# Operands laid out by the host: a two-layer streaming encoder whose cached keys, first input and some weights arrive feature-major, and whose other weights arrive in contiguous blocks

## The chip, the cores and the metric

The kernel runs on one core of a Trainium2 chip. The metric is the device time of one execution in microseconds, the median of the runs shown. All arithmetic is in 32 bits; matrix products are made from split operands (below).

## The reference, cut to what matters

Two token streams pass through the same two layers: a prompt of 512 frames, and a sample of 8 running streams with 16 new frames each, which also attends to 1024 cached positions.

```
D_MODEL = 1024; SEQ = 512; DEPTH = 2; DEC_BATCH = 8; DEC_SEQ = 16; PAST_LEN = 1024
G_A = 4; H_B = 4; NOPE_DIM = 128; ROPE_DIM = 64; Q_LORA = 384; KV_LORA = 256; H_C = 4; D_C = 64

def trunk_layer(x, q_pos, past, ...):
    p = x @ w_in
    a_u, a_v, b_cq, b_ckv, b_kr, c_q, c_k, c_v = jnp.split(p, in_split_points(), axis=-1)
    u = jax.nn.gelu(a_u); v = layer_norm(jax.nn.gelu(a_v))
    y_a = spatial_gate(u, v, w_s, b_s)                     # w_s: 4 x 128 x 128, masked by chunk
    q = jnp.einsum('bsc,chd->bshd', rms_norm(b_cq, g_cq), w_uq)
    q_rope = rope(q[..., NOPE_DIM:], q_pos)
    q_lat = jnp.einsum('bshn,hcn->bshc', q[..., :NOPE_DIM], w_uk)
    ckv = rms_norm(b_ckv, g_ckv); krope = rope(b_kr, q_pos)
    # past: cached ckv (1024 x 256), krope (1024 x 64), stick-breaking k and v (1024 x 4 x 64)
    out_lat = softmax(q_lat . ckv_all + q_rope . kr_all) . ckv_all
    y_b = jnp.einsum('bshc,hcd->bshd', out_lat, w_uv)
    y_c = stick_breaking(c_q, k_all, v_all)
    y = concat(rms_norm(y_a), rms_norm(y_b), rms_norm(y_c))
    x = layer_norm(ALPHA * x + y @ w_out)
    h = jnp.square(jax.nn.relu(x @ w_up + b_up)) @ w_down + b_down
    return layer_norm(ALPHA * x + h), caches
```

The outputs are both streams after two layers and the new cache entries.

## The kernel before, in words

**Split products.** An operand is cut into a high half, rounded by a cast on ACT, and a low half, the rest, by a subtraction on DVE or POOL (`split`). A product is then three matmuls (`mm3`: high-high, high-low, low-high). For the sample's attention, the query's high and low halves are stacked as the 128 columns of the stationary operand, so two matmuls do (`block` in `sample_scores`), and `fold_to` adds the two halves of the result.

**Transposes.** TensorE contracts over partitions, so an operand must lie with its contracted feature along the partitions. What lies otherwise is turned by TensorE: a matmul with the identity writes the turned block to PSUM (`tr` for 32-bit data, `trr` for rounded data), and the split reads it from there. In the kernel before these are turned on chip: the input of each layer (`transpose_x`), the cached keys of both attentions (`cache_T`: two blocks of 128 keys by 256 features, four transposes, then a split from PSUM), the cached rotary keys (`kr_of` and `turned`: a split in SBUF with the low half made on POOL into `kds`, four transposes, one copy to `kr`), the spatial weights (`gm_weights`, four per call), and `w_uk` for the sample's queries (`s_prep`, eight per layer), besides attention weights and activations made on chip, which stay so.

**Two threads.** The prompt (P) runs `p_layer`: phase `in` (input projection), `mix` (gating, latents and the prompt's stick-breaking attention), `mla` (`lane_pmla`), `out` and `mlp` (`p_out_mlp`). The sample (S) runs `s_layer`: it waits for P's `mix`, then `s_prep`, latent attention (`lane_smla`), stick-breaking attention (`lane_ssb`), `out` and `mlp` (`s_out_mlp`). P's phase `in` of the second layer waits for S's end of the first layer, since it projects the sample's frames too. Both threads are generators; `weave` interleaves them in one program order. It keeps a credit in estimated TensorE time: S gets `RATE[phase of P]` (0.6 to 1.0 while both run) of what P gets, where both can go on. `Pace` estimates when each engine comes to an instruction; it knows ACT, DVE, POOL and TensorE costs, no DMA. Inside a thread, `lanes` interleaves generators in the same way. The order that comes out is each engine's order; nothing is reordered at run time, apart from what the scheduler of the framework does at build time.

**Sample attention.** `pipeline` runs `front` (scores) ahead of `back` (values) by two or three pairs of sequences. Per sequence and 512 keys, `front` loads keys in two half blocks of 256 KB (ring `rawK`, two buffers), turns and splits them to `cT`, and multiplies one half block behind; `back` loads values in two half blocks (ring `rawV`, two buffers), casts the high half on DVE and subtracts the low half on POOL (`cN`). Per layer that is 32 half blocks of keys and 32 of values in each of the two attentions.

**Queues.** Every DMA is issued by SP, in program order, so a transfer that waits for its buffer holds back those behind it. `load_w` (line 258) loads weights to the rings `rawP` (three buffers, four at the start) and `rawS`, `load_cache` (line 1082) the cached keys and values. In the profile almost all engine instructions carry line 109, that of the helper `Timed`, so groups are told apart by their tiles.

## Time and profile before

| | |
|---|---|
| median of 3 runs | 1838.31 us (1836.42 to 1840.13) |
| profiled execution, span from first to last instruction | 1839.0 us |
| profiled execution, mean granted TensorE clock | 0.983 |
| TensorE matmuls | 9756, busy 95% of the span |
| DVE, ACT, POOL busy | 69%, 51%, 20% |
| bytes by DMA | 300.54 MB, queue busy 52.5% of 16 engines' span |

The profiled execution's own time is its span. A busy time is the union of the instructions' own durations; TensorE matmuls overlap in its pipeline, so the mean duration of one is longer than the distance from start to start.

### The profile page before, as it was taken

Reading aid. Unit: us, or ns where it says so; the run is one execution under the profiler, and the core shown is the slowest. Engines: PE = TensorE matmul, PEld = TensorE weight load, DVE = VectorE, ACT = ScalarE, POOL = GpSimd, SP = SyncE. Lnnn points to the kernel's source line nnn. Section 1 sums busy time; section 2 is a strip of 40 time slices with the busy share of each in tenths; the row PEclk is TensorE's granted clock in tenths of the full one; section 3 lists DMA queues with packets and bytes.
Section 4 is the critical chain, followed back from the end, with each engine's and each line's share of the span. In section 5 each row is a group of like instructions: output and inputs, shape, how many; then the busy total and the mean of one; then the engine's idle time right before and its main releaser. Section 6 shows DMA issues by size and latency. Waiting matters only on the chain.

```text
span 1839.0 us, 26468 instructions
## 1 busy us (share of the span) xinstructions
PE 1753.1 (95%) x9756; PEld 1510.5 (82%) x9756; DVE 1277.6 (69%) x1845; ACT 938.2 (51%) x1652; POOL 363.0 (20%) x372
## 2 busy tenths in 40 slices
PE   8998998999999999999989989899899999999997
PEld 7887887888888778888778988888788888878886
DVE  3476777785676766767844767777766777677676
ACT  3474666343445434656525757663443463446561
POOL 0014123461012230000110231344402113110001
PEclk9998999999999999999999989999999999999999
DMA  6325556444355347768743245573444444677772
GB/s 209 119 73 155 154 176 172 139 135 142 112 153 167 92 131 230 254 213 269 229 141 113 77 143 171 162 221 101 152 155 138 138 150 130 198 220 244 229 229 102
DMA packets 240018, 300.54 MB, mean 163 GB/s; under 512 B 35088, under 2 KB 167312, under 8 KB 239888
## 3 DMA queue, kind: packets, MB, share of 16 engines
q1 hardware_dynamic: 239888, 298.85, 52.5%
q8 instruction: 77, 1.26, 0.3%
q14 instruction: 53, 0.43, 0.1%
HBM read 281.49 MB, written 17.30 MB: 162 GB/s over the span
## 4 chain that ended last, share of the span: by engine, by line
PE 68%; DVE 11%; DMA 8%; ACT 5%; issue 5%; POOL 2%; SPq 0%; DVEq 0%; POOLq 0%; ACTq 0%
PE acc L109 47%; PE sC L109 12%; PE x L109 8%; DMA rawV<-in_cache_mla_ckv_dram 3%; DMA rawP<-in_w_down_dram 2%; DVE w L109 2%; ACT w L109 2%; POOL cN L109 2%; DVE xy L109 2%; DVE a L109 1%; DVE wx L109 1%; DVE cN L109 1%; DVE m L109 1%; DMA rawK<-in_cache_mla_ckv_dram 1%; ACT a L109 1%
## 5 line engine op out<-in xcount | busy, mean ns | idle before, releaser
L109 PE MATMUL acc<-yT,wx 128*128 128x512 f32 (+1 forms) x1632 | 395.8, 386 | 0.4 <-DVE wx L109 0.2
L109 PE MATMUL acc<-w,hT 128*128 128x512 f32 x1536 | 391.3, 397 | 1.8 <-DVE xy L109 0.9
L109 PEld LDWEIGHTS acc<-yT,wx 128*128 128x128 f32 x1632 | 292.0, 191 | 59.0 <-DVE wx L109 1.5
L109 PEld LDWEIGHTS acc<-w,hT 128*128 128x128 f32 x1536 | 283.3, 188 | 66.0 <-DVE xy L109 2.3
L109 POOL TENSOR_TENSOR cN<-rawV,cN 128x512 fp32r<-128x512 f32 x128 | 185.6, 1455 | 472.2 <-DVE cN L109 463.7
L109 DVE TENSOR_TENSOR w<-rawP,w 128x1024 fp32r<-128x1024 f32 (+4 forms) x122 | 146.9, 1206 | 136.9 <-ACT w L109 135.9
L109 DVE TENSOR_TENSOR wS<-rawS,wS 128x1024 fp32r<-128x1024 f32 x144 | 177.2, 1236 | 65.5 <-ACT wS L109 61.6
L109 ACT CAST wS<-rawS 128x1024 fp32r<-128x1024 f32 x144 | 150.9, 1051 | 116.0 <-PE sC L109 41.2
L109 PE MATMUL acc<-w,xT 128*128 128x512 f32 (+3 forms) x960 | 196.2, 358 | 8.1 <-DVE ev L109 7.9
L109 ACT CAST w<-rawP 128x1024 fp32r<-128x1024 f32 (+4 forms) x122 | 122.6, 1007 | 145.3 <-DMA rawP<-in_w_down_dram 100.8
L109 PEld LDWEIGHTS acc<-w,xT 128*128 128x128 f32 x960 | 163.1, 199 | 23.4 <-DVE ev L109 8.5
L109 DVE TENSOR_TENSOR xy<-xy,acc 128x512 f32<-128x512 f32 x128 | 85.3, 680 | 53.3 <-PE acc L109 52.9
L109 DVE CAST cN<-rawV 128x512 fp32r<-128x512 f32 x128 | 82.7, 655 | 45.4 <-DMA rawV<-in_cache_mla_ckv_dram 21.4
L109 ACT CAST cT<-sC 128x512 fp32r<-128x512 f32 x128 | 75.1, 590 | 72.5 <-PE sC L109 60.0
L109 PE MATMUL x<-wS,htS 128*128 128x512 f32 x384 | 103.9, 395 | 1.2 <-DVE htS L109 1.1
L109 POOL TENSOR_SCALAR rs<-mv 128x1 f32<-128x1 f32 x20 | 14.4, 719 | 454.4 <-DVE mv L109 453.2
L109 PE MATMUL sC<-wS,x1TS 128*128 128x512 f32 x384 | 102.4, 393 | 1.6 <-DVE x1TS L109 1.6
L109 DVE TENSOR_TENSOR cT<-sC,cT 128x512 fp32r<-128x512 f32 x128 | 87.1, 683 | 22.4 <-ACT cT L109 21.2
L109 DVE TENSOR_TENSOR wx<-rawP,wx 128x1024 fp32r<-128x1024 f32 x68 | 85.9, 1267 | 19.1 <-ACT wx L109 18.9
L109 PE MATMUL x<-cN,pTs 128*128 128x256 f32 x512 | 90.6, 290 | 4.4 <-POOL cN L109 3.3
L109 PEld LDWEIGHTS sC<-wS,x1TS 128*128 128x128 f32 x384 | 71.9, 188 | 18.1 <-DVE x1TS L109 2.1
L109 ACT CAST wx<-rawP 128x1024 fp32r<-128x1024 f32 x68 | 71.0, 1048 | 28.2 <-PE acc L109 25.1
(284 smaller groups left out, 2992.8 us busy)
## 6 DMA issues: line engine op xcount, KB each, us to landing
rawP<-in_w_up_dram SPq DMA_DIRECT2D x64, 512.0 KB
rawP<-in_w_down_dram SPq DMA_DIRECT2D x64, 512.0 KB
rawS<-in_w_up_dram SPq DMA_DIRECT2D x64, 512.0 KB
rawS<-in_w_down_dram SPq DMA_DIRECT2D x64, 512.0 KB
rawK<-in_cache_mla_ckv_dram SPq DMA_DIRECT2D x64, 256.0 KB
rawV<-in_cache_mla_ckv_dram SPq DMA_DIRECT2D x64, 256.0 KB
rawK<-in_cache_sb_k_dram SPq DMA_DIRECT2D x64, 256.0 KB
rawV<-in_cache_sb_v_dram SPq DMA_DIRECT2D x64, 256.0 KB
```

The source lines that it names most:

```text
L109: return f(out, *a, **k)
```

## The change

The host passes arrays in another layout: `t_x` (both streams' inputs, feature-major), `t_ckv` and `t_sbk` (cached keys, feature-major, in blocks of 512 keys), `t_kr` (cached rotary keys, feature-major, written twice one under the other, so 128 partitions), `t_ckvv` and `t_sbv` (cached values in blocks), `t_ws`, `t_wss`, `t_bs`, `t_bss` (spatial weights and biases for prompt and sample, the sample's spread over 8 sequences with zeros), `t_wukT` (w_uk turned), `t_wkv`, `t_win`, `t_wout`, `t_wup` (weights in blocks of one contiguous run per partition). On chip, the transposes of these operands go, with the copies from PSUM that followed them; the splits read the loaded block in SBUF. Key blocks are cut by 128 features by 512 keys instead of 256 keys by 256 features, so a score matmul has 512 columns instead of 256. The rates, the rings' depths and `Pace` are left as they are.

```diff
@@ sample_scores
-                for hf in range(2):
-                    yield at("sC")
-                    c4 = cache_T(pl, load_cache(pl, src(j, c)[:, 2 * hf:2 * hf + 2], "K", n))
-                    if late:
-                        yield at("none", late[0].args[4])
-                        late.pop(0)()
-                    if kr_of and not hf:
-                        kr = yield from turned()
-                    if s_ is None:
-                        yield at(acc)
-                        s_ = bank(acc)
-                    late.append(partial(block, j, q, s_, hf, c4, kr, c))
+                for ct in range(2):
+                    raw = half(pl, "K", n)
+                    ld.dma_start(raw, src(j, c)[:, ct])
+                    c4 = pl.tile([128, 2, 512], F32R, tag="cT", name="cT", bufs=2)
+                    split(c4[:, 0], c4[:, 1], raw)
+                    if kr_of and ct:
+                        kr = kr_of(j, c)
+                    if late:
+                        yield run(late[0])
+                        late.pop(0)()
+                    late.append(partial(block, j, q, c, ct, c4, kr))
@@ sample_scores, block
-            for ct in range(2):
-                pe.matmul(o, q[ct], c4[:, 0, ct], start=(ct == 0), stop=False)
-                pe.matmul(o, q[ct], c4[:, 1, ct], start=False, stop=(ct == 1 and kr is None))
+            pe.matmul(s_, q[ct], c4[:, 0], start=(ct == 0), stop=False)
+            pe.matmul(s_, q[ct], c4[:, 1], start=False, stop=(ct == 1 and kr is None))
@@ lane_smla, kr_of
-                krs = smp.tile([128, 4, ROPE], F32, tag="krs", name="krs")
-                ld.dma_start(krs, cache_mla_krope[l, 2 * pr + j, 512 * c:512 * c + 512].rearrange("(p k) d -> p k d", k=4))
-                kd = smp.tile([128, 4, 2, ROPE], F32R, tag="kds", name="kds")
-                split(kd[:, :, 0], kd[:, :, 1], krs, pool)
...
-                        trr(pt[:, i * 128:(i + 1) * 128], kd[:, i].rearrange("p a d -> p (a d)"))
-                    act.copy(kr, pt)
+                raw = smp.tile([128, 512], F32, tag="krs", name="krs")
+                ld.dma_start(raw, t_kr[l, 2 * pr + j, c])
+                kr = smp.tile([128, 512], F32R, tag="kr", name="kr", bufs=2)
+                act.copy(kr, raw)
+                sub(kr[64:128], raw[64:128], kr[64:128])
@@ p_layer
+            def x_first(t):
+                raw = boot.tile([128, 1024], F32, tag="xraw", name="xraw", bufs=5)
+                ld.dma_start(raw, t_x[:, t])
+                c = slice((t - 1) * 128, t * 128)
+                hi, lo = (XT[:, 0, :, c], XT[:, 1, :, c]) if t else (xS[:, 0], xS[:, 1])
+                split(hi, lo, raw.rearrange("p (k c) -> p k c", c=128))
+
+            x_first(0)
             for i, u in enumerate(units_of(O_C, 512)):
                 units.append(u)
-                if i < 3:
-                    ld.dma_start(xy[:, i + 2], x_in(i + 2))
-        for t in tiles[:3 + (l == 0)]:
-            yield at("acc")
-            x_T(t)
+                x_first(i + 1)
+        else:
+            for t in tiles[:3]:
+                yield at("acc")
+                x_T(t)
@@ gm_weights
-        yield at(tag, wsn)
-        pt = bank(tag)
-        for g in range(4):
-            tr(pt[:, g * 128:(g + 1) * 128], wsn[:, g])
@@ s_prep
-        for g in range(2):
-            yield at("sC")
-            pt = bank("sC")
-            for i in range(4):
-                h, k = 2 * g + i // 2, i % 2
-                tr(pt[:, i * 128:(i + 1) * 128], rv[:, k, h])
-            split(wuT[:, 0, 2 * g:2 * g + 2], wuT[:, 1, 2 * g:2 * g + 2], pt.rearrange("p (h c) -> p h c", c=256))
+        ld.dma_start(raw, t_wukT[l])
+        split(wuT[:, 0], wuT[:, 1], raw.rearrange("p (h c) -> p h c", c=256))
@@ p_out_mlp, wup (w_in, w_out, w_uk with w_uv alike)
-            return load_w(w_up[l, :, f * 128:(f + 1) * 128].rearrange("(k p) c -> p k c", p=128), 8, 128, om, "wx", 2)
+            return load_w(t_wup[l, f].rearrange("p (k c) -> p k c", c=128), 8, 128, om, "wx", 2)
```

## Rows read from the trace of the kernel before

**Rows 1.** The page, part 1: busy time and share of the span by engine.
```profile
PE 1753.1 (95%) x9756; PEld 1510.5 (82%) x9756; DVE 1277.6 (69%) x1845; ACT 938.2 (51%) x1652; POOL 363.0 (20%) x372
```

**Rows 2.** The page, part 4: the chain that ended last, by engine and line.
```profile
PE 68%; DVE 11%; DMA 8%; ACT 5%; issue 5%; POOL 2%; SPq 0%; DVEq 0%; POOLq 0%; ACTq 0%
PE acc L109 47%; PE sC L109 12%; PE x L109 8%; DMA rawV<-in_cache_mla_ckv_dram 3%; DMA rawP<-in_w_down_dram 2%; DVE w L109 2%; ACT w L109 2%; POOL cN L109 2%; DVE xy L109 2%; DVE a L109 1%; DVE wx L109 1%; DVE cN L109 1%; DVE m L109 1%; DMA rawK<-in_cache_mla_ckv_dram 1%; ACT a L109 1%
```

**Rows 3.** Windows: busy time by engine in stretches of the span.
```profile
core 0: us, PE busy (x) PEld busy (x) DVE busy (x) ACT busy (x) POOL busy (x), PEclk, DMA share, GB/s
...
192.00:304.00 112.00, 101.96 (x799) 96.17 (x799) 85.09 (x175) 72.44 (x170) 34.34 (x37) 0.97 0.54 167
...
430.00:560.00 130.00, 129.74 (x687) 109.67 (x687) 87.47 (x121) 61.23 (x96) 16.14 (x14) 1.00 0.45 137
...
700.00:930.00 230.00, 224.52 (x996) 182.06 (x995) 176.32 (x193) 126.31 (x170) 17.49 (x14) 1.00 0.75 239
```

**Rows 4.** Groups by tiles: operation, count | busy us, mean ns | idle before.
```profile
L109 PE MATMUL sC<-identr,rawK 128*128 128x128 f32 x512 | 80.2, 277 | 4.7 <-DVE cT L109 3.0 <-DMA rawK<-in_cache_sb_k_dram 0.8 <-DMA rawK<-in_cache_mla_ckv_dram 0.5
...
L109 PE MATMUL sC<-cT,qlT 128*128 128x256 f32 x256 | 50.7, 301 | 4.8 <-DVE cT L109 4.6
...
L109 PE MATMUL x<-cT,qS 128*128 128x256 f32 x256 | 46.1, 292 | 0.9 <-DVE o L109 0.5 <-ACT cT L109 0.3
...
L109 PE MATMUL sC<-kr,qrS 128*128 128x256 f32 x64 | 18.2, 284 | 0.3 <-ACT kr L109 0.3
L109 PE MATMUL sC<-identr,kds 128*128 128x128 f32 x128 | 15.9, 247 | 0.1
```

**Rows 5.** Timeline, TensorE: start us, length of the run in us, tiles, count.
```profile
26.31 1.03 PE L109 MATMUL acc<-identr,xy 128*128 128x128 f32 x8
...
200.97 1.67 PE L109 MATMUL acc<-ckT,w 128*128 128x256 f32 x12
...
212.94 0.46 PE L109 MATMUL sC<-identr,kds 128*128 128x128 f32 x4
...
1815.10 14.26 PE L109 MATMUL acc<-w,hT 128*128 128x512 f32 x60 [0.31 <-DVE xy L109]
```

**Rows 6.** Single tiles (rawK, kds, w): ns of one matmul, minimum, median, maximum.
```profile
L109 PE MATMUL sC<-identr,rawK x512: 270/272/476, 197.8 to 1499.4; 128*128 128x128 f32 x171
...
L109 PE MATMUL sC<-identr,kds x128: 222/248/455, 198.5 to 1263.0; 128*128 128x128 f32 x128
...
L109 PE MATMUL acc<-w,hT x1536: 387/393/503, 413.5 to 1829.0; 128*128 128x512 f32 x192
...
L109 PE MATMUL acc<-cqT,w x144: 277/281/387, 183.4 to 1179.4; 128*128 128x256 f32 x144
```

**Rows 7.** Single tiles (cT, hT): ns of one DVE subtraction, minimum, median, maximum.
```profile
L109 DVE TENSOR_TENSOR cT<-sC,cT x128: 660/683/693, 200.0 to 1506.8; 128x512 fp32r<-128x512 f32 x128
...
L109 DVE TENSOR_TENSOR hT<-relu,hT x64: 670/684/1781, 405.5 to 1808.6; 128x512 fp32r<-128x512 f32 x64
```

**Rows 8.** Groups by tiles: DVE and POOL subtractions, busy us, mean ns.
```profile
L109 POOL TENSOR_TENSOR cN<-rawV,cN 128x512 fp32r<-128x512 f32 x128 | 185.6, 1455 | 472.2 <-DVE cN L109 463.7 <-DMA rawV<-in_cache_sb_v_dram 3.7 <-PE acc L109 2.0
...
L109 DVE TENSOR_TENSOR hT<-relu,hT 128x512 fp32r<-128x512 f32 x64 | 50.3, 787 | 12.9 <-ACT hT L109 12.8
```

**Rows 9.** Waits of SP, the DMA queue: waiter, released by, us in total, times, longest.
```profile
SPq L1082 <- POOL cN L109: 185.5, 105, 7.9
SPq L1082 <- PE sC L109: 141.3, 73, 14.4
```

**Rows 10.** Timeline of the start: the first projection, and its last weight block.
```profile
14.13 4.18 PE L109 MATMUL acc<-w,xS 128*128 128x512 f32 x12
...
16.37 1.05 ACT L109 CAST w<-rawP 128x1024 fp32r<-128x1024 f32 x1 [0.70 <-DMA rawP<-in_w_in_dram]
```

**Rows 11.** Timeline, TensorE, end of layer one: the sample's last product.
```profile
918.40 5.27 PE L109 MATMUL x<-wS,htS 128*128 128x512 f32 x20 [1.08 <-DVE htS L109]
```

**Rows 12.** The page, part 2: DMA packets, bytes, packets by size.
```profile
DMA packets 240018, 300.54 MB, mean 163 GB/s; under 512 B 35088, under 2 KB 167312, under 8 KB 239888
```

More of the change, by code (lines that the diff above doesn't have):

```diff
@@ L204, in x_in @@
         return x_sample.rearrange("b s d -> (b s) d") if t == 0 else x_prompt[0, (t - 1) * 128:t * 128]
-    for t in range(2):
-        ld.dma_start(xy[:, t], x_in(t))
-    blocks = cp.tile([128, NB], F32, name="blocks")
-    ld.dma_start(blocks, c_block)
     mhalf = cp.tile([128, 4, 4], F32, name="mhalf")
@@ L679, in load_wkv @@
         raw = stage("P")
-        for i, src in enumerate((w_uk, w_uv)):
-            for k in range(2):
-                ld.dma_start(raw.rearrange("p (i k h n) -> p i k h n", i=2, k=2, h=2)[:, i, k],
-                             src[l, 2 * a:2 * a + 2, k * 128:(k + 1) * 128].rearrange("h p n -> p h n"))
+        ld.dma_start(raw, t_wkv[l, a])
         w = wp.tile([128, 2, 1024], F32R, tag="w8", name="w8", bufs=4)
@@ L1103, in sample_scores, with run, block @@
     def sample_scores(pl, s2, src, q_of, new, msk, n, kr_of=None, kr_new=None):
[L1106 removed]
+        late, held = [], []
         acc = "sC" if kr_of else "x"
[L1109 to L1117 removed]
+        def run(f):
+            return at("none" if f.args[3] else acc, *(x for x in f.args[4:] if x is not None))
+        def block(j, q, c, ct, c4, kr):
+            if ct == 0:
+                held.append(bank(acc))
+            s_ = held[0]
+            pe.matmul(s_, q[ct], c4[:, 0], start=(ct == 0), stop=False)
+            pe.matmul(s_, q[ct], c4[:, 1], start=False, stop=(ct == 1 and kr is None))
+            if ct:
+                if kr is not None:
+                    pe.matmul(s_, q[2], kr, start=False, stop=True)
+                fold_to(s2[64 * j:64 * j + 64, 512 * c:512 * c + 512], held.pop(), 512, pl)
         def fresh(j, q, s_):
@@ L1475 @@
         "ln1_g", "ln1_b", "w_up", "b_up", "w_down", "b_down", "ln2_g", "ln2_b"]
+_LAID = {"cache_mla_ckv", "cache_mla_krope", "cache_sb_k", "cache_sb_v", "w_in", "w_s", "b_s", "w_uk", "w_uv", "w_out"}
 _OUTS = [(1, 512, 1024), (8, 16, 1024), (2, 1, 512, 256), (2, 1, 512, 64), (2, 1, 512, 4, 64), (2, 1, 512, 4, 64),
@@ L1517 @@
     given = {n: _np.ascontiguousarray(inputs[n]) for n in _INS}
+    laid = _laid_out(given)
+    given = {n: given[n] for n in _INS if n not in _LAID}
     given.update(_constants())
+    given.update(laid)
     for name, a in given.items():
```

138 lines of the change are left out of this document (65 added, 73 removed).

## The prediction

> **What bounds the kernel now.** I read the busy times first, then the chain of waits, then the stretches, and only then single tiles. TensorE's matmuls cover 95% of the span, DVE 69%, ACT 51%, POOL 20% [rows 1]. A busy TensorE alone would prove little, but the chain that ended last runs through it for 68% of the span, with DVE at 11% and DMA at 8% [rows 2]. The reader should see in the stretches where this holds and where it does not [rows 3]. While the prompt is in its MLP and the sample in its stick-breaking attention (430 to 560 us), TensorE is busy 129.74 of 130 us and DVE 67%. In the two MLPs (700 to 930) TensorE has 98%, DVE 77%, DMA 0.75. While both threads are in latent attention (192 to 304, and alike in the second layer) TensorE has 102 of 112 us, but DVE 85 and ACT 72: there two engines are close to each other, and that is the stage to watch. Everywhere else a TensorE instruction that goes is time that goes, since both threads are woven into one stream and the other thread's matmuls move up.
>
> So each removed matmul has to be priced by the distance from start to start in a dense run, not by its own duration. A run of n takes n-1 distances and one duration. Eight 32-bit transposes took 1.03 us [rows 5] and one lasts 0.272 [rows 6], so the distance is (1.03-0.272)/7 = 0.108 us. For rounded transposes (0.46-0.248)/3 = 0.071; for 256 columns (1.67-0.281)/11 = 0.126; for 512 columns (14.26-0.393)/59 = 0.235, from the same two groups. The busy column of the groups (80.2 us for the 512 key transposes [rows 4], 0.157 each) counts a part of the next instruction's time with it and is not used.
>
> **The change part by part, on TensorE.**
> - Cached keys: 512 transposes [rows 4] go, 512 x 0.108 = 55.3 us.
> - Rotary keys: 128 transposes [rows 4] go, 128 x 0.071 = 9.1 us.
> - Scores: 256 + 256 + 64 matmuls of 256 columns [rows 4] become 288 of 512: 576 x 0.126 - 288 x 0.235 = 72.6 - 67.7 = 4.9 us. Merging pays only the small overhead of an instruction; the columns stay.
> - First input: 5 tiles x 8 transposes go, 40 x 0.108 = 4.3 us. They stand in front of everything.
> - Spatial weights (4 in each of 4 calls) and w_uk (8 in each layer): 32 x 0.108 = 3.5 us.
>
> Together 77.1 us. By the Trainium skill, "TensorE: Matmul & The Clock Gate", Part 4, a transpose took about 275 ns in one kernel's context; by that price the 712 transposes would be an estimated 196 us. The trace has the same duration for one, 0.272 us, and shows beside it that eight in a row cost 0.108 each, so the sum above stays; the other reading is a rival below.
>
> **On the other engines, and what hides it.** ACT's 128 casts of keys stay and read SBUF in place of PSUM; for rotary keys one cast of 256 columns goes; for the first input ten casts of 512 become five of 1024. ACT is at 51% and has cover in every stretch. DVE's 128 key subtractions stay (0.683 us [rows 7]) and 32 are added for the rotary keys, at the same length 21.9 us, some 8 of them in the stretch 192 to 304; POOL loses the 32 of the rotary keys. DVE's cover is TensorE's time in the same stretch; where it is gone, each costs its full length.
>
> There is one price that the trace of before shows only at a distance. A key subtraction reads PSUM now and never took over 0.693 us in 128 [rows 7]. It will read two operands in SBUF, as the subtraction to hT does, which has the same median (0.684) but a maximum of 1.781 [rows 7] and a mean of 0.787 [rows 8]; and POOL subtracts the values' low halves in the same stages, 185.6 us in all [rows 8]. So each key subtraction loses between 0 and 1.1 us; I take hT's mean excess of 0.10, because that row has the same shape and operands, 13 us of DVE over the whole span. The Trainium skill, "SBUF — State Buffer", says of the shared port pair that a DVE instruction with two SBUF inputs contends with a GpSimd instruction that reads SBUF, and that the second to start blocks fully. The two rows of DVE agree with it; it speaks against this change, and its case is a rival below.
>
> What these do to the path: in 192 to 304 TensorE's work falls by about 14 us (92 of the 799 are key transposes, by the pattern 23 half blocks, 10 us, and 3 for rotary keys), to 98 or less with the waits in it, while DVE's rises from 85 to about 96 (8.2 and 23 x 0.10). The two are then equally loaded, and more steps wait for each other. Between nothing and the whole 14 us can be given back there per layer; I take 5, nearer the lower end since the sample's work that is then late can run in the next stretch, where DVE has a third of its time free. For two layers 10 us.
>
> **On the queue.** A key buffer is now freed by its transposes; SP waited for those 141.3 us in 73 waits [rows 9]. After the change it is freed by the DVE subtraction, later by a cast (half of the 1.05 us that 1024 columns take [rows 10]) and a subtraction (0.68) less four transposes (3 x 0.108 + 0.272 = 0.60), 0.6 us for each of 128 half blocks or 77 us of queue time, with the weights' transfers queued behind. The chain has key transfers for 1% of the span [rows 2], 18 us beside 141 waited, so between 0 and 77 x 18/141 = 10 us come to the path. I take 0, as the split is now started before the previous block's matmuls are waited for, and keep 10 for the range. Values move as before. Rotary keys are loaded twice over: 32 x 128 KB more, 4.2 MB of 300; at DMA shares of 0.45 to 0.75 [rows 3] that is covered. Of the packets 167312 of 240018 are under 2 KB [rows 12]; the contiguous blocks make them larger, most of all for w_up, but the chain has no line of w_up, w_in or w_out [rows 2], so I count nothing for it. Four DMAs for w_uk and w_uv become one, and the small pieces for spatial weights go; nothing on the chain waits for them.
>
> **At the start.** The first projection begins at 14.13 us, and the last of its four weight blocks reaches ACT at 16.37 [rows 10], behind five inputs. In the new order it comes eighth of nine transfers instead of last, and a projection can start when one input and one block are split. The 4.3 us above are counted; a further 0 to 4 us may come, I take 0.
>
> **The sum.** 1839.0 - 77.1 + 10 = 1771.9 us for the profiled execution. The median of the runs shown is 0.7 us below that execution (1838.31), so the forecast is 1771 us.
>
> **The rivals.**
> - *More than the matmuls goes.* TensorE's own waits for the keys' splits and transposes are 4.7 + 4.8 + 0.9 + 0.3 us [rows 4], the start has up to 4 and key transfers are on the chain for 18. Without any giveback: 1839 - 77 - 11 - 4 = 1747, and 1735 if much of the 18 goes too. For it: fewer steps between landing and product. Against it: a new wait usually takes the place of an old one. Chance 0.14 (1735 to 1755).
> - *Late keys and uneven threads.* The queue's 10 us, the latent stage's other 18 us, and the threads' ends: the sample's last product of layer one ends at 923.7 [rows 11], close to the prompt's last, because the rates fit the old work. If the sample keeps its pace in clock time while the prompt runs ahead, the sample's MLP ends alone: a lead of some 35 us per layer leaves about half of that, 12 weight blocks of six matmuls (1.4 us) each, and at the 239 GB/s of that stretch [rows 3] a block of 524 KB takes 2.2 us, so 12 x 0.8 = 10 us are idle. All together 1771 + 38 = 1809. Chance 0.18 (1790 to 1810).
> - *The change doesn't free the path.* DVE, not TensorE, sets the attention stages, and they stay as long as they are; only the start gets shorter: 1834 to 1839. Against it: TensorE's 129.74 of 130 us. Chance 0.04.
> - *Slower by the shared port.* Each key subtraction collides with a value subtraction on POOL, on which the value matmuls wait. It decides from 77/128 = 0.6 us per key half block that comes through to TensorE; at 0.8 us it would be 1839 - 77 + 102 = 1864. For it: the maximum of 1.781 us. Against it: hT's mean excess is 0.10, and POOL is busy 34 of 112 us in that stage [rows 3]. Chance 0.06.
> - *Transposes cost their full duration.* If 0.272 us each were on the path, 712 x 0.272 = 194 us, less 5 for the scores and with 10 back: 1650. Against it: the run of eight. Chance 0.02.
>
> **How the numbers follow.** The forecast's own case, 1755 to 1790 us, has 0.56. The range reaches into the better and the late case until about 2 in 10 is left out: 1742 to 1806. A measurement of this kernel can tell about 0.2%, 3.7 us, from no change. Faster: 0.56 + 0.14 + 0.18 + 0.02 = 0.90; the same 0.04; slower 0.06.
>
> **What would show it.** Matmuls fall from 9756 by 712 + 288 to about 8756. TensorE stays above 93% busy in 430 to 560; the key groups have no transposes, and the scores' group has half the count with 512 columns. In latent attention DVE's share comes near TensorE's, and idle time before the scores is put down to DVE cT or to a DMA of rawK: if it exceeds 10 us per layer, the giveback was set too low. If cT's maximum is far above 0.69 us, the port is shared as feared; if its mean stays under 0.8, it costs little. If layer one does not end some 30 us earlier, the threads have come apart. A time above 1810 or below 1735 would say that the price per transpose, or the engine that bounds the stages, was misread.

## The result, and the profile after

The changed kernel took **1861.35 us** (median; 1859.09 to 1872.37), beside 1838.41 for the kernel before on the same chip: ratio 1.0136, 95% interval 1.0106 to 1.0166. The forecast was 1771 and faster; it is slower by 23 us. The profiled execution took 1858.5 us, 19.5 more than that of before.

The page, part 1, of the changed kernel, and three of its windows (TensorE, its weight loads, DVE, ACT and POOL busy, the granted clock, DMA share, GB/s):

```profile
PE 1724.9 (93%) x8756; PEld 1460.2 (79%) x8756; DVE 1307.1 (70%) x1870; ACT 931.0 (50%) x1613; POOL 342.6 (18%) x338
```
```profile
192.00:304.00 112.00, 95.39 (x544) 84.42 (x544) 96.93 (x187) 72.61 (x154) 25.61 (x19) 0.85 0.60 185
430.00:560.00 130.00, 125.30 (x577) 101.31 (x576) 106.42 (x137) 72.52 (x108) 21.81 (x14) 0.98 0.45 144
700.00:930.00 230.00, 218.97 (x970) 178.06 (x968) 160.38 (x177) 116.39 (x160) 8.78 (x14) 0.98 0.64 202
```

Exactly the expected 1000 matmuls are gone [rows 1]. Their time is not: in 192 to 304 us TensorE runs 544 matmuls where it ran 799 [rows 3], and is still busy for 95 of 112 us. A good part of this is its mean granted clock (the share of full speed that it was given), which is 0.85 there in place of 0.97. DVE rose from 85 to 97 us and is now the busiest engine of that stretch.

To see where the 19.5 us arise, the span is cut at two instants per layer that both kernels have: the first product of the prompt's latent attention (`acc<-w,cqT`) and the first of its MLP (`acc<-yT,wx`). What lies between is called **the stage** below. The single tiles give the instants (minimum, median, maximum ns, then first and last start in us), first for the kernel before, in layer one and two, then for the changed one:

```profile
L109 PE MATMUL acc<-w,cqT x72: 220/276/415, 177.1 to 255.4; 128*128 128x128 f32 x72
L109 PE MATMUL acc<-yT,wx x605: 274/393/550, 381.0 to 699.8; 128*128 128x512 f32 x128, 128*128 128x256 f32 x24
...
L109 PE MATMUL acc<-w,cqT x72: 220/275/415, 1090.4 to 1167.5; 128*128 128x128 f32 x72
L109 PE MATMUL acc<-yT,wx x696: 274/393/541, 1293.8 to 1699.5; 128*128 128x512 f32 x150, 128*128 128x256 f32 x24
```
```profile
L109 PE MATMUL acc<-w,cqT x72: 221/301/415, 175.7 to 267.6; 128*128 128x128 f32 x72
L109 PE MATMUL acc<-yT,wx x552: 274/393/562, 393.4 to 698.8; 128*128 128x512 f32 x152, 128*128 128x256 f32 x32
...
L109 PE MATMUL acc<-w,cqT x72: 222/276/415, 1095.0 to 1193.4; 128*128 128x128 f32 x72
L109 PE MATMUL acc<-yT,wx x624: 274/392/796, 1318.6 to 1657.8; 128*128 128x512 f32 x132, 128*128 128x256 f32 x24
```

The second layer's projection starts at 930.9 before and 930.1 after (first start of `acc<-w,xT`). That gives the account:

| part of the span, us | before | after | difference |
|---|---|---|---|
| layer one, up to the stage | 177.1 | 175.7 | -1.4 |
| layer one, the stage | 203.9 | 217.7 | +13.8 |
| layer one, the rest | 549.9 | 536.7 | -13.2 |
| layer two, up to the stage | 159.5 | 164.9 | +5.4 |
| layer two, the stage | 203.4 | 223.6 | +20.2 |
| layer two, the rest | 545.2 | 539.9 | -5.3 |
| sum | 1839.0 | 1858.5 | +19.5 |

So the gain came where the prompt is in its MLP, but only 18.5 us of it, and the latent attention stage took 34 us more. The stage's windows, before and after:

```profile
177.00:381.00 204.00, 187.60 (x1334) 171.89 (x1334) 155.87 (x283) 115.22 (x251) 66.42 (x63) 0.97 0.52 157
1090.00:1294.00 204.00, 188.58 (x1357) 171.79 (x1357) 155.91 (x295) 117.93 (x260) 65.69 (x65) 0.99 0.51 158
```
```profile
176.00:393.00 217.00, 187.88 (x1089) 163.45 (x1089) 175.51 (x311) 113.04 (x238) 63.28 (x52) 0.90 0.52 160
1095.00:1319.00 224.00, 191.56 (x1105) 166.04 (x1106) 175.58 (x311) 116.05 (x245) 63.86 (x55) 0.90 0.49 154
```

The reader should see three things. TensorE has some 250 matmuls less in the stage and it got longer. DVE has 20 us more, and the stage grew by 14 and 20. And DVE's idle time in it hardly moved: 48 and 48 us before, 42 and 48 after. Two sources of DVE's 20 us show in the groups and tiles: the rotary keys' subtractions (16 in layer one's stage, 12.9 us), and the sample's progress: it starts its stick-breaking scores 66 us after the prompt's MLP started before (447.4 to 381.0), and only 18 after it now (411.0 to 393.4), so work that ran beside the MLP runs inside the stage.

The waits of the trace say what TensorE's idle time in the stage was put down to. It was 16 and 15 us before, of which 13 and 12 by DVE, 3 and 2 by ACT, 1 and 0 by POOL; it is 29 and 32 after, of which 15 and 22 by DVE, 8 and 9 by ACT, 5 and 2 by POOL. DVE has the largest part, but the waits for ACT and POOL grew as well.

### The profile page after: what moved, and what is told of

It reads as the page before. It is cut to its first block, busy times and chain, and to the rows that moved or that the text cites. A ratio compares the mean times of both kernels' runs of the same rounds, so it can differ in the third digit from the quotient of the medians.

```text
span 1858.5 us, 24372 instructions
## 1 busy us (share of the span) xinstructions
PE 1724.9 (93%) x8756; PEld 1460.2 (79%) x8756; DVE 1307.1 (70%) x1870; ACT 931.0 (50%) x1613; POOL 342.6 (18%) x338
## 2 busy tenths in 40 slices
DMA packets 145817, 305.05 MB, mean 164 GB/s; under 512 B 32032, under 2 KB 46496, under 8 KB 145696
## 5 line engine op out<-in xcount | busy, mean ns | idle before, releaser
L109 PE MATMUL acc<-w,hT 128*128 128x512 f32 x1536 | 399.5, 401 | 6.7 <-DVE xy L109 3.9
L109 PEld LDWEIGHTS acc<-yT,wx 128*128 128x128 f32 x1632 | 298.4, 194 | 68.1 <-ACT wx L109 3.7
L109 PEld LDWEIGHTS acc<-w,hT 128*128 128x128 f32 x1536 | 288.7, 191 | 75.0 <-DVE xy L109 6.4
L109 POOL TENSOR_TENSOR cN<-rawV,cN 128x512 fp32r<-128x512 f32 x128 | 196.2, 1538 | 605.9 <-DVE cN L109 584.8
L109 ACT CAST cT<-rawK 128x512 fp32r<-128x512 f32 x128 | 78.7, 620 | 54.9 <-DMA rawK<-in_t_sbk_dram 17.8
L109 DVE TENSOR_TENSOR cT<-rawK,cT 128x512 fp32r<-128x512 f32 x128 | 93.7, 738 | 16.2 <-ACT cT L109 15.5
L109 PEld LDWEIGHTS x<-cN,pTs 128*128 128x128 f32 x512 | 78.9, 195 | 23.0 <-POOL cN L109 9.4
L109 DVE CAST cN<-rawV 128x512 fp32r<-128x512 f32 x128 | 73.2, 578 | 27.7 <-PE x L109 14.9
```

What stands on the lines that cost most here:

```text
L109: return f(out, *a, **k)
```

## The experiments

The theories, by the letters that the expectations use: **A**, the loss is made in the latent attention stage, into which the sample's blocks are now emitted faster; **B**, a cost that both attentions share (late key transfers, the port of DVE and POOL); **C**, the contiguous blocks; **D**, DVE is what ends last in that stage; **E**, casts that wait for keys in ACT's queue; **F**, the prompt's chain alone sets the stage; **G**, the granted clock in its own right. Except where said, each kernel is the changed kernel with the edit shown.

### Which part of the change costs the time

**The latent keys transposed again, and then the stick-breaking keys.** Their blocks are loaded key-major and turned by the loop of before:

```diff
-            yield from sample_scores(smp, s2, keys(pr), q_of, cnT, ...)
+            yield from turned_scores(smp, s2, values(pr), q_of, cnT, ...)   # the loop of before
```


> Theory A (latent attention is the place: there the sample's key blocks, without their transposes and the two yields that went with them, are emitted faster into a stretch where DVE and ACT are already full, and TensorE waits more than it saved): with the latent keys transposed again, and only they, the stretch from 186 to 300 us goes back to about what it was before, and the stick-breaking keys still save 256 x 0.108 us + 2 for scores, with the first input and the small weights some 37 us in all, so about 1795 to 1810. Rival B (something that both attentions share: late key transfers, or the port of DVE and POOL): half of the loss stays, about 1840 to 1855. Rival C (the contiguous weight blocks or the new order of transfers cost the time, not the keys): 1855 to 1885.

> The mirror of the run before it: only the stick-breaking keys are transposed again. Theory A: the loss stays whole and the saving there goes, 1861 + 30 = about 1885 to 1895. Rival B (a cost that both attentions share): half of the loss goes with half of the saving, 1840 to 1860. Rival C (the weight blocks): 1885 to 1895 too, so it is told apart by the other run.

Measured: 1839.72 us (ratio to before 1.0011, 0.9989 to 1.0034) and 1875.82 (1.0227, 1.0202 to 1.0252). Against the changed kernel, transposing the latent keys again makes it 22 us *faster*, transposing the stick-breaking keys again 14 us slower. B, which expected the same sign from both, falls, although the first run alone stands at the edge of its range; the second lies in no theory's range. C, which expected no gain from the first, falls as the whole cause. A's place holds, but its size does not: 1840 is far from 1800.

**The whole latent attention as before,** rotary keys included (`kds` split by POOL and turned by four rounded transposes):

> The whole of the sample's latent attention as before: its keys and also its rotary keys are loaded key-major and transposed on chip, the rotary low halves made by POOL; all else as in the changed kernel. Theory A (the loss is made in the latent attention stage, where the prompt's chain over DVE and ACT and not TensorE sets the length; the run with the latent keys alone turned back still had the 32 rotary subtractions on DVE and a denser order, 1840): the stage from the start of the prompt's latent attention to its MLP goes from 218 and 224 us back to about 204 in each layer, the stick-breaking keys save their 28 us elsewhere, 1800 to 1820. Rival B (something that every laid-out key pays): 1835 to 1850.

Measured: 1832.46 us (0.9975, 0.9950 to 1.0000). The stage came back, to 196.6 and 206.9 us, with DVE at 151 us:

```profile
176.00:372.00 196.00, 179.51 (x1289) 163.56 (x1289) 151.17 (x273) 109.05 (x239) 63.74 (x60) 0.99 0.50 158
1078.00:1285.00 207.00, 189.93 (x1319) 172.32 (x1318) 151.82 (x282) 114.16 (x250) 66.42 (x64) 0.96 0.48 151
```

The total missed A's range by 12 us. So part of the stick-breaking gain is lost elsewhere, and the next run shows one possible place.

**Only the weights and the first input laid out** (all keys of both attentions transposed):

> All cached keys transposed on chip as before (rotary keys too); only the weights' contiguous blocks, the first input, the spatial weights and w_uk laid out. By the prices of the prediction 4.3 + 3.5 us go: 1828 to 1834. If the new blocks and the order of the transfers cost something themselves (rival C): above 1840.

Measured: 1845.59 us (1.0054, 1.0030 to 1.0079), 9 us slower than before (1836.85 beside it) where 8 were expected as a gain. That is C's side of the expectation: the layout of the weights, or the order that comes with it, has a cost of its own. In layer two the stage starts 169 us after the projection instead of 159.5. I took it for w_uk's missing step and put that back, in this kernel (`seam`) and later in the fastest version (`best_seam`):

```diff
-        split(wuT[:, 0], wuT[:, 1], raw.rearrange("p (h c) -> p h c", c=256))
+        for g in range(2):
+            yield at("sC")
+            pt = bank("sC")
...
+                tr(pt[:, i * 128:(i + 1) * 128], rv[:, k, h])
+            split(wuT[:, 0, 2 * g:2 * g + 2], wuT[:, 1, 2 * g:2 * g + 2], pt.rearrange("p (h c) -> p h c", c=256))
```


> The run with only weights and first input laid out (1846, where 1830 was expected) with w_uk key-major again: loaded so and turned by 8 transposes per layer, as before. In that run the sample's preparation moved ahead of the prompt's first latent products, which started 168.8 us into layer two where they had started 159.5 before. If the missing w_uk step is what moved them: the prompt starts there at 158 to 162 again and the time is 1832 to 1840. If something else of the layout costs it (blocks of w_in, spatial weights): 1843 to 1850, start still at 166 or later.

> The fastest version so far (1824) with w_uk transposed on chip as before. If w_uk's step is what costs the seam: 1812 to 1820. If not: 1822 to 1832.

Measured: 1856.39 us (1.0108, 1.0083 to 1.0133), with the stage of layer two still 166 us after the projection; and 1822.95 (0.9936, 0.9911 to 0.9960) beside 1824 without it. w_uk is not it: a step nearer to the kernel before was 11 us worse. That left the order itself, and one run for it.

**The kernel before with two rates changed:**

```diff
-RATE = {..., 'mla0': 1.0, ..., 'mla1': 0.9, ...}
+RATE = {..., 'mla0': 0.9, ..., 'mla1': 0.8, ...}
```


> The kernel before with nothing but two of the rates changed that decide the order (the sample's share while the prompt is in latent attention, 1.0 and 0.9, become 0.9 and 0.8): the same instructions, of which only the order of the two threads differs; the sample comes out some 15 us further ahead in the first layer, about half of what the changed kernel does. If the kernel before owes part of its time to an order that fits its work (and any change of the work draws a new one): 1844 to 1860. If the order is worth little: within 4 us of 1838.

Measured: 1845.67 us (1.0045, 1.0029 to 1.0060). The same instructions in another order cost 8 us. So the kernel before owes some of its time to an order that fits its work, and a change of the work draws a new one. From this one run I estimate that single differences below some 10 us are within what a new order can do. Whether the layout's 9 us come from the order or from the new transfers was not found.

### What sets the stage

**Transposes without use.** If TensorE's removed work had lain on the path, putting it back must cost it:

```diff
                     ld.dma_start(raw, src(j, c)[:, ct])
+                    idle = ps.tile([128, 512], F32, tag="sC", name="sC", bufs=BUFS["sC"])
+                    for i in range(4):
+                        nc.tensor.transpose(idle[:, i * 128:(i + 1) * 128], raw[:, i * 128:(i + 1) * 128], ident)
```


> The changed kernel with four transposes of each raw key block back on TensorE, into a PSUM tile that nothing reads; they are not entered in the estimate that sets the order and have no yield, so the order is that of the changed kernel. Theory A (order): the stick-breaking half costs its 28 us, the latent half some part of its 28 since TensorE has idle time there, 1885 to 1915. Rival (the granted clock falls in the latent attention only because TensorE has too little to do, and that is the whole loss): the clock is back at full and the time falls to 1835 to 1860.

With `if kr_of:` ahead of the added lines, in latent attention alone:

> The changed kernel with four transposes of each raw key block back on TensorE in latent attention alone, into a PSUM tile that nothing reads, with neither an entry in the order's estimate nor a yield: 256 x 0.108 = 28 us of TensorE work without use. Theory D or F (TensorE work in that stage is covered, and its clock falls there because it waits): within 8 us of 1861, above or below, with fewer microseconds at half clock. If the TensorE work of this stage still lay on the path: 1885 or more.

Measured: 1869.45 us (1.0196, 1.0160 to 1.0231) for 512 added transposes, 55 us of TensorE work by the prediction's price, so 8 more than the changed kernel; and 1855.06 (1.0103, 1.0077 to 1.0129) for the 256 of latent attention, 28 us of work, not more than the changed kernel. For the first, A's range was 15 us too high, and the clock's, that ended at 1860, too low. The stages of the first run, then of the second:

```profile
180.00:403.00 223.00, 195.33 (x1224) 172.52 (x1224) 172.55 (x310) 113.34 (x238) 62.96 (x52) 0.94 0.49 154
1114.00:1340.00 226.00, 198.29 (x1228) 173.72 (x1229) 174.73 (x309) 114.17 (x240) 60.76 (x53) 0.93 0.49 152
```
```profile
178.00:391.00 213.00, 188.54 (x1220) 165.99 (x1220) 171.79 (x310) 112.32 (x238) 62.83 (x52) 0.97 0.51 164
1098.00:1315.00 217.00, 193.13 (x1202) 169.59 (x1202) 172.49 (x308) 112.98 (x238) 61.43 (x53) 0.93 0.50 158
```

Against the changed kernel there are 100 to 140 more matmuls in the stage, some 14 us of work by the same price. In the second run its length is 213 and 217 us, a little less; in the first, with the same transposes in this stage, it is 223 and 227, a little more (its profiled execution, 1880 us, was the slowest of its four). So the added work cost between nothing and 5 us per stage. But it brought clock with it: in the second run the stage is at 0.97 and 0.93 instead of 0.90, and TensorE's busy time stayed at 189 and 193 us. By the two levels of the clock, full and half, 43 and 45 us of the changed kernel's stage were at the lower one, and 13 and 30 are here. Half of what went, 15 and 8 us, is TensorE's time given back, about what the added work needed. So these runs alone don't tell a stage that TensorE doesn't bound from one in which the lower clock had eaten the saving, and that the transposes of the kernel before had been free there is not shown.

**The prompt alone.** The sample's two attentions, its output projection and its MLP are left out:

```diff
-        yield from lane_smla(l, ql)
...
-        yield from lane_ssb(l)
...
-        yield from s_out_mlp(l)
+        pool.memset(xy[:, 0, 256:], 0.0)
+        ln2["S"] = pace.t
+        flags.add(f"done{l}")
+        ld.dma_start(xscr[:, 0] if l < L - 1 else o_ys.rearrange("b s d -> (b s) d"), xy[:, 0])
```


> The sample's two attentions, its output projection and its MLP are left out; the prompt does all its work. It measures how long the prompt's latent attention and output projection take by themselves; with the sample beside them they took 204 and 203 us before and 218 and 224 in the changed kernel, of which TensorE needs some 95 for the prompt's own products. Theory F (the prompt's chain over DVE and ACT alone sets this stage, and TensorE work of the sample in it is free): 180 us or more. Theory D (DVE shared by both threads sets it): 130 to 165, with DVE's share far below the 86 of 114 us that it has with the sample. If TensorE set it: under 125.

```profile
175.00:322.00 147.00, 125.70 (x768) 109.92 (x768) 90.36 (x163) 58.06 (x129) 15.14 (x19) 0.94 0.29 90
873.00:1021.00 148.00, 126.49 (x763) 109.97 (x763) 89.89 (x162) 57.61 (x129) 15.72 (x20) 0.94 0.27 86
```

Measured: 1399.73 us (one execution), a stage of 146 and 148 us, in D's range. F falls: the sample's work lengthens the stage, before by 57 us for 66 us of DVE work (156 less 90), after by 71 to 76 for 85. That is some 0.85 us of stage per us of DVE, as a ratio: the sample brings TensorE and ACT work at the same time (62 and 57 us in layer one before), so this run doesn't single out DVE. DVE's idle time is 57 and 58 us here, against 42 to 48 with the sample.

**DVE work moved to POOL,** first the rotary low halves, then also every second low half of the latent keys:

```diff
-                sub(kr[64:128], raw[64:128], kr[64:128])
+                sub(kr[64:128], raw[64:128], kr[64:128], pool)
```
```diff
-                    split(c4[:, 0], c4[:, 1], raw)
+                    split(c4[:, 0], c4[:, 1], raw, pool if kr_of and ct else None)
```


> The changed kernel with the 32 low halves of the rotary keys made by POOL, as before, in place of DVE (22 us of DVE work in all, 11 in each latent attention). Theory D (in that stage DVE is what ends last): most of it comes back, 1840 to 1850. Rival (order or clock alone, DVE has room): 1855 to 1865.

> As the run before it, and every second key half block of the latent attention has its low half made by POOL as well: 43 us less on DVE than in the changed kernel, some 70 more on POOL, a quarter busy there. Theory D (DVE ends last): 1820 to 1840. Rival (order or clock alone): 1855 to 1870, or above where POOL's 1.46 us in place of 0.68 make the keys late.

Measured: 1858.29 us (1.0109, 1.0092 to 1.0127) and 1838.56 (1.0006, 0.9989 to 1.0023). The first misses D's range: DVE fell by 7 and 9 us and the stage by 2 and 11, but the other parts of the span grew by 13, so alone it settles nothing. The second is in D's range, 23 us below the changed kernel with the same matmuls and POOL's slower subtraction in place of DVE's; the rows show DVE down by 17 and 14 us and the stage by 12 and 7. In layer two TensorE's clock and busy time are those of the changed kernel, so the 7 us there are not the clock's; in layer one the clock came up from 0.90 to 0.93 as well:

```profile
179.00:384.00 205.00, 178.46 (x1071) 155.77 (x1071) 158.95 (x278) 112.55 (x237) 105.05 (x82) 0.93 0.53 168
1086.00:1303.00 217.00, 189.61 (x1102) 163.71 (x1103) 161.58 (x280) 114.76 (x243) 106.88 (x85) 0.90 0.51 162
```

**The order of the sample's blocks.** In latent attention one yield more per key half block, and 1.3 us of TensorE time entered that nothing uses:

```diff
                     ld.dma_start(raw, src(j, c)[:, ct])
+                    if kr_of:
+                        yield at("sC")
+                        pace.add("pe", 1.3, raw.tensor.name, [])
```


> Work as in the changed kernel; in latent attention the emitter yields once more for each key half block and enters 1.3 us of TensorE time that is not used, so that the sample's blocks are spread over more of the prompt's work, in about the order of the kernel before. Theory A: the stretch of the latent attention loses most of its waits, 1765 to 1810. Rivals (late keys, port of DVE and POOL, casts that wait in ACT's queue): these costs per key block stay wherever the block stands, 1845 to 1870.

Measured: 1833.45 us (0.9978, 0.9955 to 1.0000), 28 below the changed kernel with the same work. The costs per block are thus not the whole story, as the rivals had it, but A's 1765 to 1810 is missed as well. DVE's work in the stage fell by 16 and 14 us since the sample's blocks spread into the prompt's MLP, and the stage by 19 and 12.

**The split one block later:**

```diff
-                    split(c4[:, 0], c4[:, 1], raw)
...
+                    step = partial(halves, j, q, c, ct, raw)
+                    if held_back:
+                        yield from held_back.pop()()
+                    held_back.append(step)
```


> The changed kernel with the cast and the subtraction of each key half block emitted one block after its load, so that ACT's queue does not stand in front of a transfer that has not landed. Theory E (the wait for the keys, formerly TensorE's, now stands in ACT's in-order queue ahead of the prompt's evacuations): 1800 to 1835. Theories A and D: within 10 us of 1861.

Measured: 1856.78 us (1.0100, 1.0080 to 1.0120). E falls.

The stage over the kernels (both layers; matmuls, DVE busy and idle from the windows, length from the tiles):

| kernel | matmuls in it | DVE busy, us | length, us | DVE idle, us |
|---|---|---|---|---|
| before | 1334, 1357 | 156, 156 | 204, 203 | 48, 48 |
| changed | 1089, 1105 | 176, 176 | 218, 224 | 42, 48 |
| latent keys transposed | 1278, 1298 | 169, 172 | 213, 209 | 44, 38 |
| latent attention as before | 1289, 1319 | 151, 152 | 197, 207 | 45, 55 |
| unused transposes, latent | 1220, 1202 | 172, 172 | 213, 217 | 41, 44 |
| unused transposes, both attentions | 1224, 1228 | 173, 175 | 223, 227 | 50, 51 |
| rotary halves on POOL | 1095, 1091 | 168, 166 | 216, 212 | 48, 46 |
| and key halves on POOL | 1071, 1102 | 159, 162 | 205, 217 | 46, 55 |
| sample's blocks spread | 1015, 1024 | 160, 162 | 199, 211 | 39, 49 |
| prompt alone | 768, 763 | 90, 90 | 146, 148 | 57, 58 |

The length follows DVE's busy time, with 38 to 58 us on top in every row, and not the matmuls: 1015 of them took 199 us and 1289 took 197. A caution: a stage that is long for another reason also takes in more of the sample's DVE work. The runs that change a stage's load at unchanged work elsewhere are what speaks for a direction: TensorE's up, from 7 us shorter to 5 longer, with the clock up; DVE's down and POOL's up, 2 to 12 us shorter. No run adds work to DVE alone, which would be the direct test of D.

### A faster version, and what is left in it

Both remedies together, the blocks spread by 1.3 us in layer one and 0.9 in layer two:

> The changed kernel with the two remedies together, each of which alone gave back 23 to 28 us: half of the latent keys' low halves and the rotary ones on POOL, and the sample's key blocks spread by an unused 1.3 us (first layer) and 0.9 us (second layer) of TensorE time each in the estimate. If they mend different things (DVE's load, the order): 1800 to 1822. If both mend the same wait: 1828 to 1840.

Measured: 1825.98 us (0.9935, 0.9909 to 0.9961); between the two expectations, and faster than both kernels. From here, three single additions: the unused latent transposes (`best_warm`), all latent low halves on POOL (`pool if kr_of else None`, `best_e`), and every second low half in both attentions on POOL (`pool if ct else None`, `best_f`):

> The faster version (spread blocks, half of the latent keys' low halves on POOL; 1826) with the four unused transposes of each latent key block added, 28 us of TensorE work. In the changed kernel the same addition did not cost anything (1855 against 1861) while the time at half clock fell from 174 to 119 us. Theory G (the low clock carries what is left: with more to do TensorE keeps its clock): below 1826, 1812 to 1824. Theory D (the clock only follows from waits on DVE; with DVE relieved, TensorE's work begins to count again): 1830 to 1850.

> The faster version with all low halves of the latent keys on POOL instead of every second one: 22 us less on DVE, 47 more on POOL, which is then some two thirds busy in that stage. Theory D (DVE still ends last there): 1808 to 1822. If POOL's slower subtraction becomes the next wait: 1828 to 1845.

> The faster version with every second low half of the stick-breaking keys on POOL as well (22 us less on DVE, 47 more on POOL). In that stage DVE is 81% busy and TensorE 96 to 98%. If the stick-breaking half of the expected gain (28 us, of which the run with the latent attention undone shows 13) is lost to DVE too: 1808 to 1820. If not: within 6 us of 1826.

Measured: 1826.40 us (0.9922, 0.9897 to 0.9946), 1840.97 (1.0013, 0.9997 to 1.0030) and 1824.25 (0.9917, 0.9895 to 0.9940). The stages of `best_a` and `best_warm`, and then of `best_e`:

```profile
178.00:377.00 199.00, 174.24 (x1024) 151.24 (x1024) 147.22 (x259) 106.34 (x225) 96.34 (x77) 0.92 0.51 165
1078.00:1283.00 205.00, 177.52 (x1065) 154.63 (x1066) 154.61 (x268) 112.49 (x238) 99.80 (x79) 0.93 0.52 165
```
```profile
180.00:383.00 203.00, 183.74 (x1153) 162.76 (x1152) 147.70 (x257) 108.52 (x226) 104.19 (x78) 0.94 0.51 162
1077.00:1285.00 208.00, 184.56 (x1191) 162.82 (x1190) 158.03 (x264) 110.73 (x235) 99.55 (x79) 0.96 0.51 159
```
```profile
180.00:385.00 205.00, 175.38 (x1007) 151.73 (x1007) 135.44 (x240) 104.04 (x221) 112.16 (x90) 0.88 0.50 158
1104.00:1302.00 198.00, 172.40 (x1028) 149.91 (x1029) 142.52 (x242) 106.30 (x224) 116.06 (x92) 0.93 0.52 164
```

`best_warm` lies in neither range. G falls for this version: the clock came up and no time was gained. D's number falls too: 28 us of TensorE work more didn't change the total, although less clock came back for it than in `filler_lat`. The stage itself grew by 4 us per layer, so TensorE counts there in part, and the rest of the span made up for it.

With all low halves on POOL, DVE has 135 and 143 us in the stage, but the stage stays at 205 and 199, DVE is idle for 70 and 55 us of it, and POOL has 112 and 116. So the length no longer follows DVE's load there. The subtraction takes about twice as long on POOL, and the time is in the range that was given for POOL as the next wait; that POOL ends last was not tested apart. Stick-breaking halves on POOL are within the change of order.

## Why the prediction was wrong

**The step that failed is the give-back in latent attention:** "Between nothing and the whole 14 us can be given back there per layer; I take 5". Both the bound and the value took TensorE's time as the ground from which something is lost, so the worst case was a stage as long as before. The runs showed a longer one: with some 250 matmuls less the stage grew by 14 and 20 us. By the prediction's own prices 39 us of latent keys, rotary keys and their scores, less the 10 given back, were to be gained there, and 34 were lost. That is 63 of the 87 us between the sum of 1771.9 and the profiled 1858.5; 11 more are missing in the rest of the two layers and 12 ahead of the stages.

What stands in its place: the stage is not as long as TensorE's work. Some 20 us came to DVE there, and taking 17 and 14 us off DVE again made it 12 and 7 us shorter with the same matmuls (`split_pool`). The prediction had said "DVE's cover is TensorE's time in the same stretch; where it is gone, each costs its full length", and had DVE rising from 85 to 96 in 192 to 304, as it did (97); but a bound that ends at "nothing gained" left out that the stage can become longer. DVE's 85 of 112 us [rows 3] was read as room. The prompt alone leaves DVE idle for 57 us of this stage, in a chain that hops between engines (by the waits of layer one, 27 us for ACT and 24 for TensorE). With the sample beside it 38 to 55 us of idle time remained in the rows of the table, 48 in the kernel before, so little room was left to fill.

How much of the 34 us is DVE's is argued, not shown. No run adds work to DVE alone, the waits for ACT and POOL grew beside those for DVE, and the lower clock of TensorE in this stage (*The clock*, below) is not separated from it.

Point by point:

- *The price of the matmuls* held. Giving every matmul of both traces the 30th percentile of the start-to-start distances of its shape, the stream falls from 1680 to 1603 us, by the 77 that were forecast. What is left of the span, waits and low clock, rose from 159 to 256.
- *The clock* was not in the sum. By the mean granted clock and its two levels of 1.2 and 2.4 GHz, 2 x (1 - 0.983) x 1839 = 63 us were at the lower level before and 175 after; in the stage, by the windows, 12 and 4 us before and 43 and 45 after. In the changed kernel's trace matmuls of 128 columns are 0.213 us apart at the lower level and 0.108 at the upper (30th percentile), so half of the added time, 16 and 20 us, is an estimate of what the clock took from TensorE there. It is as much as the stage grew, and TensorE's busy time in it didn't fall (188 and 189 us before, 188 and 192 after). The clock fell where TensorE waits more, so I take it to follow from the waits, but that it costs nothing in the changed kernel is not shown. Against it as the whole cause stand `best_warm`, where it came up and gained nothing, and layer two of `split_pool`, 7 us shorter at the same 0.90. The Trainium skill, "TensorE: Matmul & The Clock Gate", section "HAM oscillation — how this bites in real kernels", advises to leave TensorE no long idle gaps so that its clock stays up; the trace of `filler_lat` agrees for the clock (0.953 to 0.968). With unused work as the filling the time hardly followed: 6 us there, nothing in `best_warm`.
- *Stick-breaking keys and MLP*: the right direction, less than half the size. The rest of the two layers gained 18.5 us, where the 28 of these keys alone were expected. With the transposes gone the sample runs faster there too, and DVE comes near to TensorE:

```profile
1330.00:1460.00 130.00, 129.35 (x687) 109.09 (x686) 88.51 (x122) 59.22 (x95) 18.01 (x15) 1.00 0.49 147
1460.00:1600.00 140.00, 139.50 (x720) 117.06 (x719) 96.32 (x126) 63.58 (x100) 32.86 (x22) 1.00 0.52 150
```
```profile
1330.00:1460.00 130.00, 125.98 (x606) 104.42 (x607) 108.15 (x143) 74.72 (x117) 33.73 (x17) 0.97 0.49 156
1460.00:1600.00 140.00, 133.58 (x613) 108.76 (x612) 86.83 (x110) 56.44 (x87) 29.06 (x20) 0.96 0.48 154
```

  The first two rows are of before, the others of the changed kernel: in 270 us of layer two TensorE's idle time goes from 1 to 10 us, 9 of the 14 us expected in that layer. What else holds it back was not isolated.
- *The threads* came apart, but the other way round than the rival had it: the sample ran ahead, not the prompt. The sample's last product of layer one ends at 870 us, where it ended at 924 [rows 11], and the prompt is alone at the end of the layer (TensorE 49 of 60 us busy from 870 on, where it had 54.5).

```profile
868.79 1.07 PE L109 MATMUL x<-wS,htS 128*128 128x512 f32 x4
```

- *Order* was taken as given ("the other thread's matmuls move up"). `b_rate` shows that it is worth 8 us with the same instructions, and the laid-out weights alone lost 9 where 8 were forecast as a gain. The first projection did start 6.8 us earlier (first start of `acc<-w,xS` at 7.4 where it was 14.1), but the stage only 1.4.
- *The shared port* cost DVE less than was taken. The changed kernel's subtractions of keys and rotary keys, beside [rows 7]:

```profile
L109 DVE TENSOR_TENSOR cT<-rawK,cT x128: 654/684/2881, 187.2 to 1474.9; 128x512 fp32r<-128x512 f32 x128
...
L109 DVE TENSOR_TENSOR kr<-krs,kr x32: 689/690/1655, 189.4 to 1233.6; 64x512 fp32r<-64x512 f32 x32
```

  The maximum rose to 2.881 us but the mean only to 0.738 (93.7 us in 128), 7 us in all, where 13 were taken. POOL's value subtractions beside them grew from 1455 ns [rows 8] to 1538, 10.6 us in all. In the stage (DVE busy with the tile cT, the clock, DMA share, GB/s; two rows of before, two of the changed kernel) the key subtractions took no longer in layer one and 3 us longer in layer two:

```profile
177.00:381.00 204.00, 21.85 (x32) 0.97 0.52 157
1090.00:1294.00 204.00, 21.89 (x32) 0.99 0.51 158
```
```profile
176.00:393.00 217.00, 21.54 (x32) 0.90 0.52 160
1095.00:1319.00 224.00, 25.13 (x32) 0.90 0.49 154
```

  What the Trainium skill says in "SBUF — State Buffer", section "SBUF: two separate sides", of an exclusive pair of ports that a DVE instruction with two SBUF inputs shares with POOL, fits the maxima. These rows rule it out for the key subtractions as what made the stage 14 and 20 us longer.
- *The queue*: taken as 0. Casts held back by a block changed the time by 5 us, which an order can do; no run shows a loss by late keys.
- *The rivals*: "The change doesn't free the path" named DVE, with a chance of 0.04 and no loss in its price. The slower rival named the port; that its 1864 is close to the measured 1861 is luck. Of the signs, "if it exceeds 10 us per layer, the giveback was set too low" did not come: the idle time before the latent scores is 10 us in both layers together, most of it put down to ACT.

```profile
L109 PE MATMUL sC<-cT,qlT 128*128 128x512 f32 x128 | 52.0, 471 | 10.0 <-ACT cT L109 8.2 <-DVE cT L109 1.6
```

  So the sign looked at the sample's scores alone, while the idle time grew all over the stage. The last sign came: a time above 1810, and "the engine that bounds the stages, was misread".

## What to carry to other kernels

Work that goes from an engine is a gain only in the stretches where that engine ends last; for each stretch, take the busy time of every engine, and compare its idle time with what the stretch has when one thread runs alone: an engine at 76%, as DVE in the stage before, can have little room left. Before removing work, put unused work of the same kind *in*, and look at the granted clock beside the time: where it costs nothing at an unchanged clock, expect little from taking work away. (Here this was done afterwards and on the changed kernel alone, and the clock moved with it.) And where two threads are woven by estimated costs, a change of the work changes the order, here worth 8 us with no other difference, so rates and the placing of work on engines have to be set anew with the change (here from 1861 to 1824).

## What the runs showed that was not expected

- 256 transposes added to the changed kernel did not make it slower (1855 against 1861; the intervals of the two ratios overlap), while TensorE's granted clock came up from 0.953 to 0.968.
- The prompt alone, with no key or value work of the sample on POOL, has no stretched DVE subtraction in its MLP: the hT subtraction, up to 1.781 us with the sample [rows 7], takes at most 0.695.

```profile
L109 DVE TENSOR_TENSOR hT<-relu,hT x64: 682/693/695, 340.9 to 1368.3; 128x512 fp32r<-128x512 f32 x64
```

- Contiguous blocks took the DMA packets from 240018 [rows 12] to 145817, at the same bandwidth (163 and 164 GB/s), and no run shows a gain by it.
